# Three Strassen stages of an encoder block: products that run on in shared PSUM banks, weights two k tiles to an instruction, one weight sum by an accumulating DMA

## The chip, the core and the metric

The kernel runs on one core of a Trainium2 chip. The metric is the device time of one launch in microseconds. The engines in the text: TensorE (PE in rows; PEld is its weight load), VectorE (DVE), ScalarE (ACT), GpSimd (POOL, which here also issues some DMAs), SyncE (SP, which issues most DMAs).

## The reference

One transformer block on 512 tokens of 2048 features, in float32; the output is its final RMSNorm.

```
a = rms_norm(h);  z = a @ w_in            # 5120 columns: queries, keys, values, two gMLP halves
h = h + [diff_attention(z) | gmlp_spatial_gate(z)] @ w_out
f = rms_norm(h)
h = h + (silu(f @ ffn_w1) * (f @ ffn_w3)) @ ffn_w2      # 5632 hidden columns
h = h + (p @ pl_w_up) * sigmoid(h @ pl_w_gate)          # "gate stage" below
out = rms_norm(h, final_norm_g)
```

## The kernel before

**Split operands.** TensorE multiplies float32r. Each operand is split into a high part (ScalarE's cast, `split`, line 114) and the exact remainder (VectorE's subtraction, line 115). A product is three matmuls: high by high, low by high, high by low. The tokens' operand is stationary (128x128), the weights move past it (128x512).

**Strassen stages.** Three stages compute 2x2 blocks by Strassen-Winograd's seven products, in `winograd` (line 198): the gMLP half of w_in ("x" stage, 2 groups of 512 columns of each block), the FFN's w1 and w3 (11 groups), and the gate's matrix (`w_gate`, 2 groups). The rest (`gemm`, line 150) is plain and does not change. A group has 7 products over 8 k tiles of 128 rows, both token halves: 7 x 8 x 2 x 3 = 336 matmuls, 56 steps of 6. `steps` fixes the order: a leading product and lagging ones that use the same loaded tile, (0),(1); (2),(3,4); (5),(6). Which engine executes what in which order is this trace order, moved forward by `tc.high_priority` and held back by `following`; each engine takes its instructions strictly in order.

**What a step needs.** `prepare` (line 250) loads a 128x512 weight tile (`raw`, SP's queue), forms a weight sum where the product wants one (`sub`, line 239, VectorE), and splits into `whi`, `wlo`. It runs `ahead` steps before the product, and a tile waits until its buffer is free again. Per k tile VectorE forms four weight sums: T1 = B12 - B11, T2 = B22 - T1, T3 = B22 - B12, T4 = B21 - T2. In the x and gate stages B12 is loaded a second time for T3 (`lean`).

**What follows a product.** A product fills one PSUM bank pair `c` (128x1024). `combine` (line 350) sums them outside TensorE: two ScalarE copies, five VectorE sums with PSUM (line 346), and two sums of SBUF tiles (line 346 too, on VectorE in the x and FFN stages, on GpSimd in the gate stage, argument `urgent`). `finish` follows each block: the FFN's Silu and product, or in the gate stage (line 1004) sigmoid (L1017), times `p @ pl_w_up` (L1018), plus h (L1020), squares for the last norm (L1052), a scaling by the norm's gain of the first blocks (`scale_up`, L1069), and the final scaling and store (`final`, L1085). In the gate stage GpSimd does L1020 and L1069 and part of L1018, VectorE the rest. In the last group the last product runs one token half after the other (`late`), so that the first half can finish earlier.

**Gate stage's start.** `gate_op` builds the stationary operand of the last two pairs of k tiles from h inside the stage (L191 and L115 on VectorE, 128x256 and 128x512).

Of the kernel before, what the change touches and what calls it, by code (L numbers as in the profile page):

```python
# [19 lines left out]
P = 128  # L20
# [31 lines left out]
class Lazy:  # L52
    """The items of a list from one on, some of which are yet to come."""
# [8 lines left out]
def block_kernel(ctx: ExitStack, tc: tile.TileContext, out, xT, pT, w_in, w_vg, w_out, w13, w2,  # L62
# [16 lines left out]
    ngain = const.tile([P, KT], F32, name="ngain")  # L79
    nc.vector.tensor_scalar(out=ngain, in0=gain[:, 0], scalar1=-1.0, scalar2=None, op0=ALU.mult)  # L80
# [54 lines left out]
    def gemm(w, op, evac, pg, before=None):  # L135
        """w: DRAM [128, nk, 256]; op: nk tiles [128, 2, 512]; evac(m, psum [128, 512])."""
# [33 lines left out]
    def moving7(pool, bufs, tmp, src, scales):  # L170
        """src: [128, 2, 512], a pair of k tiles -> [128, 7, 2, 256] in the products' order."""
# [27 lines left out]
    def winograd(wps, bp, tp, pp, op, w, ahead, lean, late, done, at, extra=None):  # L199
        """w: DRAM [groups, 128, 4, 8, 512], blocks B11, B12, B21, B22; done(g, i, psum, later)  # L200
        follows the i-th product of group g; at: what else follows which step.
        op: for each pair of k tiles, (product, part, half) -> stationary [128, 128].
        lean: loads what it can again. late: the last group does the first half of the tokens first.
        extra: a plain product before it all, (operand, DRAM [n, 128, nk, 512], evac), with
        evac(n, half of the tokens, psum)."""
        ng = w.shape[0]
        steps = []
        if extra:
            eop, ew, evac = extra
            steps = [(-1, f, k) for f in range(ew.shape[0]) for k in range(ew.shape[2])]  # L210
# [15 lines left out]
        def load(src, name, bufs):  # L226
            t = (bp if name == "b12" else wps[0]).tile([P, T], F32, name=name, bufs=bufs)
# [15 lines left out]
        def halves():  # L243
            return tuple(wps[1].tile([P, T], F32R, name=n, bufs=ahead + 1) for n in ("whi", "wlo"))

        def prepare(g, i, c):
            if g < 0:
                x = load(ew[i, :, c], "raw", RAWS)
            elif i == 0:
                x = raw(g, 0, c, "raw", RAWS)  # L250
                t1 = tp.tile([P, T], F32, name="t1", bufs=KP + SKEW)
                held[c] = [t1, b12(g, c)]
            elif i in (2, 5):
                x = raw(g, 3 if i == 2 else 2, c, "raw", RAWS)
                held[c][2:] = [x]
# [928 lines left out]
```

## Time and profile before

| | us |
|---|---|
| three runs | 2266.6, 2267.86, 2268.9; median 2267.86 |
| profiled execution: span, first to last instruction | 2266.5 |
| its first stage: normalised input, queries and keys of one head | 8.7 to 87.6 |
| x stage (Strassen) | 87.6 to 244.9 |
| other columns of w_in, attention, gMLP, w_out | 244.9 to 676.1 |
| product of p, FFN's first stage (Strassen) | 676.1 to 1576.4 |
| FFN's second product | 1576.4 to 2065.9 |
| gate stage (Strassen) | 2065.9 to 2254.0 |
| last scaling and stores | 2254.0 to 2266.5 |

The profile has no time of this execution other than its span; it lies 1.4 us under the median. Stages are cut where the lines of TensorE's matmuls change. In a timeline row the bracket is the engine's idle time just ahead of it and what released it; in a wait row, A <- B says that A's engine stood until B was done.

### The profile page before, as it was taken

To read this page: it belongs to the slowest core of one execution; us is meant where nothing else is said; L and a number is where in the kernel's file an instruction comes from. 1 tells how busy PE (TensorE), PEld (TensorE's weight loads), DVE (VectorE), ACT (ScalarE), POOL (GpSimd) and SP (SyncE) were. 2 spreads that over 40 slices of the span, in tenths; PEclk is the share of its full clock that TensorE was granted. 3 is DMA by queue.
4 is the path that set the end of the run, shared out by engine and by line. 5 is a ranking of instruction groups with operands and counts; after the bars stand their busy time and mean duration, and the time that the engine had idled before them with its cause. 6 is when DMAs were issued, how large, how long until landed. Compare 5 with 4: busy or idle time off the path is not lost. (4 is left out here: it accounts for less than half of the span.)

```text
span 2266.5 us, 27314 instructions
## 1 busy us (share of the span) xinstructions
PE 2211.0 (98%) x9714; PEld 1789.6 (79%) x9714; DVE 1547.4 (68%) x2243; ACT 995.2 (44%) x1591; POOL 175.4 (8%) x166
## 2 busy tenths in 40 slices
PE   7999999999999999999999999999999999999986
PEld 5788777878887888888888888887888888887764
DVE  8688754564539888887887888788333333556888
ACT  6355333453425545545544554555222222334544
POOL 4000300001210000000000000000000000000243
PEclk9999999999999999999999999999999999999998
DMA  5455522224436443444344344433543343545554
GB/s 167 158 154 159 198 93 75 84 75 148 142 125 215 120 140 108 120 126 127 104 122 127 111 121 118 129 107 119 177 152 120 106 141 97 151 131 165 154 163 158
DMA packets 133656, 300.57 MB, mean 133 GB/s; under 512 B 14560, under 2 KB 20192, under 8 KB 133520
## 3 DMA queue, kind: packets, MB, share of 16 engines
q1 hardware_dynamic: 110384, 245.94, 36.4%
q0 software_dynamic: 8672, 30.60, 4.0%
q10 hardware_dynamic: 14464, 22.30, 2.8%
q8 instruction: 76, 1.25, 0.2%
q14 instruction: 60, 0.49, 0.1%
HBM read 265.49 MB, written 33.29 MB: 132 GB/s over the span
## 5 line engine op out<-in xcount | busy, mean ns | idle before, releaser
L314 PE MATMUL c<-whi,op 128*128 128x512 f32 x3344 | 1051.6, 396 | 4.1 <-ACT whi L114 4.1
L314 PEld LDWEIGHTS c<-whi,op 128*128 128x128 f32 x3344 | 627.4, 189 | 145.7 <-ACT whi L114 5.8
L114 ACT CAST whi<-raw 128x512 fp32r<-128x512 f32 (+1 forms) x545 | 406.1, 747 | 717.3 <-PE ps L150 437.2
L115 DVE TENSOR_TENSOR wlo<-raw,whi 128x512 fp32r<-128x512 f32 (+1 forms) x545 | 466.2, 859 | 349.7 <-ACT whi L114 343.0
L314 PE MATMUL c<-wlo,op 128*128 128x512 f32 x1680 | 663.8, 396 | 17.2 <-DVE wlo L115 17.2
L150 PE MATMUL ps<-gop,whi 128*128 128x512 f32 x1408 | 435.4, 390 | 1.0 <-DVE c L346 1.0
L314 PEld LDWEIGHTS c<-wlo,op 128*128 128x128 f32 x1680 | 316.9, 189 | 98.4 <-DVE wlo L115 26.4
L150 PE MATMUL ps<-op,whi 128*128 128x512 f32 x1088 | 346.7, 399 | 0.0
L114 ACT CAST whi<-t 128x512 fp32r<-128x512 f32 x356 | 219.5, 620 | 213.4 <-PE c L314 143.5
L150 PEld LDWEIGHTS ps<-gop,whi 128*128 128x128 f32 x1408 | 263.2, 188 | 54.8 <-ACT gop L114 1.2
L115 DVE TENSOR_TENSOR wlo<-t,whi 128x512 fp32r<-128x512 f32 x352 | 245.1, 703 | 78.5 <-ACT whi L114 76.5
L150 PE MATMUL ps<-gop,wlo 128*128 128x512 f32 x704 | 274.4, 390 | 0.8 <-DVE wlo L115 0.8
L150 PEld LDWEIGHTS ps<-op,whi 128*128 128x128 f32 x1088 | 202.5, 188 | 44.3 <-issue 2.7
L150 PE MATMUL ps<-op,wlo 128*128 128x512 f32 x544 | 214.2, 394 | 0.0
L239 DVE TENSOR_TENSOR t<-raw,t 128x512 f32<-128x512 f32 x240 | 172.8, 721 | 46.6 <-DMA raw<-w 22.4
L150 PEld LDWEIGHTS ps<-gop,wlo 128*128 128x128 f32 x704 | 132.2, 188 | 29.0 <-DVE wlo L115 1.6
L150 PEld LDWEIGHTS ps<-op,wlo 128*128 128x128 f32 x544 | 102.1, 188 | 23.4 <-issue 1.1
L346 DVE TENSOR_TENSOR c<-c,c 128x1024 f32<-128x1024 f32 x91 | 111.0, 1220 | 10.2 <-PE c L314 10.2
L114 ACT CAST whi<-b 128x512 fp32r<-128x512 f32 x120 | 74.7, 623 | 90.4 <-PE c L314 78.7
L115 DVE TENSOR_TENSOR wlo<-b,whi 128x512 fp32r<-128x512 f32 x120 | 82.8, 690 | 18.2 <-ACT whi L114 16.2
L934 POOL DMA_DIRECT2D gl<-gd x17 | 12.3, 724 | 1056.2 <-ACT whi L114 723.6
L239 DVE TENSOR_TENSOR b<-raw,b 128x512 f32<-128x512 f32 x120 | 84.4, 704 | 5.6 <-DMA b<-w_vg 3.1
(173 smaller groups left out, 1378.4 us busy)
## 6 DMA issues: line engine op xcount, KB each, us to landing
raw<-w SPq DMA_DIRECT2D x264, 256.0 KB, 2.7
raw<-w SPq DMA_DIRECT2D x64, 512.0 KB, 3.6
b<-w SPq DMA_DIRECT2D x88, 256.0 KB, 2.9
raw<-w_in SPq DMA_DIRECT2D x40, 512.0 KB, 3.6
raw<-w_out SPq DMA_DIRECT2D x32, 512.0 KB, 3.6
raw<-w_vg SPq DMA_DIRECT2D x48, 256.0 KB, 2.7
raw<-w SPq DMA_DIRECT2D x32, 384.0 KB, 3.2
raw<-w_gate SPq DMA_DIRECT2D x48, 256.0 KB, 2.8
```

What stands on the lines that cost most here:

```text
L114: recent[:] = (nc.scalar.copy(out=hi, in_=src), nc.vector.tensor_tensor(out=lo, in0=src, in1=hi.bitcast(F32), op=ALU.subtract))
L115: nc.vector.tensor_tensor(out=lo, in0=src, in1=hi.bitcast(F32), op=ALU.subtract))
L150: nc.tensor.matmul(ps[:, m], lhsT=a[:, j, ms], rhs=op[k][:, b], start=k == 0 and i == 0, stop=k == nk - 1 and i == 2)
L239: nc.vector.tensor_tensor(o, x, y, op=ALU.subtract)
L314: product[:] = [nc.tensor.matmul(acc[i][:, s], lhsT=op[c](i, x, s), rhs=y, start=c == 0 and k == 0, stop=c == KP - 1 and k == 2)]
L346: (eng or nc.vector).tensor_tensor(o, x, y, op=ALU.add)
L934: nc.gpsimd.dma_start(out=t, in_=gd[k:k + 2].rearrange("k p t -> p k t"))
```

## The change

**Order and size.** Weights come two k tiles at a time: every load, sum and split is 128x1024, and a step is 12 matmuls, 28 steps to a group. The products' order is (0,1), (2,3), (4,5), 6, the second of a pair one step behind the first; `ahead` is 2 of these steps. Buffers: three raw tiles, three pairs of halves (`nhalf`), but two pairs in the gate stage. There, the last product's halves for c of 2 and 3 lie in B12's buffers.

**Banks that run on.** With changed signs of the operands, products accumulate where another left off: 0, 2, 4, 6 in one bank pair, 1 and 3 in a second, 5 alone. So the pair of bank 0 holds in turn what c11, c12 and c21 need. ScalarE copies c11, c22, c12 after products 0, 1, 2; VectorE adds to c12, c22, c11 after 3, 4, 5; c21 is read straight from PSUM by the activation that follows.

**Weight sums.** VectorE forms three per pair. The fourth, B12 + B22, is made in B12's tile by a DMA that GpSimd issues and that adds B22 from memory to the tile (line 266 after); B12 isn't loaded twice any more.

**Gate stage.** L1018's and L1020's successors (998, 999) and `scale_up` (1045) run on VectorE, 128x1024 each; GpSimd keeps only the power of the final norm. The gains' load goes to ScalarE's queue. The buffer for GpSimd's DMA descriptors shrinks to 4096 bytes.

The core of the diff (what lies between is renaming, docstrings, buffers and signs):

```diff
         for g in range(ng):
-            for lead, lag in (((0,), (1,)), ((2,), (3, 4)), ((5,), (6,))):
-                skew = KP if late and g == ng - 1 and lead == (5,) else SKEW
-                for c in range(KP + skew):
-                    steps += [(g, i, c) for i in lead if c < KP]
-                    steps += [(g, i, c - skew) for i in lag if c >= skew]
+            for lead, lag in ((0, 1), (2, 3), (4, 5), (6, None)):
+                for c in range(kw + (lag is not None)):
+                    if c < kw:
+                        steps.append((g, lead, c))
+                    if lag is not None and c:
+                        steps.append((g, lag, c - 1))
         todo = {}
         now = 0
...
-        def halves():
-            return tuple(wps[1].tile([P, T], F32R, name=n, bufs=ahead + 1) for n in ("whi", "wlo"))
+        def halves(i=0, c=0):
+            return tuple(
+                (bp.tile([P, 2, T], F32R, name=n, tag="b12", bufs=kw) if i == 6 and late and
+                 c >= nhalf else hp.tile([P, 2, T], F32R, name=n, bufs=nhalf)) for n in ("whi", "wlo"))
...
+            if g < 0:
+                return o
+            if i == 0:
+                sub(held[c][0], held[c][1], x)
+            elif i == 2:
+                nc.gpsimd.dma_start(out=held[c][1], in_=w[g, :, 3, 2 * c:2 * c + 2],
+                                    accum_op=ALU.add)
+            elif i == 5:
                 sub(held[c][0], x, held[c][0])
-                if i == 2:
-                    if lean:
-                        held[c][1] = b12(g, c)
-                    sub(held[c][1], x, held[c][1])
-            if g >= 0 and i > 0:
...
-            multiply(0, c, hi, lo)
+                acc[i] = bank() if i in (0, 1, 5) else acc.pop(i - 2)
+
+            def multiply(s, c, whi, wlo, p):
+                for e in range(2):
+                    k = 2 * c + e
+                    for x, y in ((0, whi), (1, whi), (0, wlo)):
+                        product[:] = [nc.tensor.matmul(
+                            p, lhsT=op[k](i, x, s), rhs=y[:, e],
+                            start=k == 0 and i in (0, 1, 5) and (x, y) == (0, whi),
+                            stop=k == KP - 1 and y is wlo, skip_group_check=True)]
...
-                    done(g, i, acc[i][:, 1], later, 1)
+                kept.append((c, whi, wlo))
+                if c == kw - 1:
+                    for s in range(2):
+                        for a in kept:
+                            multiply(s, *a, acc[i][:, s])
+                        done(g, i, acc[i][:, s], later, s)
             else:
-                multiply(1, c, hi, lo)
-                if c == KP - 1:
-                    done(g, i, acc.pop(i), later)
+                for s in range(2):
+                    multiply(s, c, whi, wlo, acc[i][:, s])
+                if c == kw - 1:
+                    done(g, i, acc[i], later)
             for fn, a in at.pop(now, []) + todo.pop(now, []):
                 fn(*a)
...
         def done(g, i, acc, later, s=slice(None)):
-            if i == 0:
-                nc.scalar.copy(out=new("c11"), in_=acc)
-            elif i == 1:
-                nc.scalar.copy(out=new("c22"), in_=acc)
-            elif i == 2:
-                add(new("c21"), acc, res["c11"])
-            elif i == 3:
-                add(new("c12"), acc, res["c21"])
-                later(2, add, res["c12"], res["c12"], res["c22"], eng)
-                later(5 if g == urgent else 3, finish, g, "c12", res["c12"], later)
-            elif i == 4:
...
+            if i < 3:
+                nc.scalar.copy(out=new(("c11", "c22", "c12")[i]), in_=acc)
+            elif i < 6:
+                n = ("c12", "c22", "c11")[i - 3]
+                add(res[n], acc, res[n])
+                later(1, following if g == last else (lambda fn, *a: fn(*a)), finish, g, n, res[n],
+                      later)
+            else:
+                if s in (0, slice(None)):
+                    new("c21")
+                with tc.high_priority(10 * PRIO) if g == urgent else nullcontext():
+                    finish(g, "c21", res["c21"], later, s, acc)
 
         return done
 
...
             nc.sync.dma_start(out=h, in_=hnat[f, u])
-            parts = [(s, o[:, s], h[:, s]) for s in range(2)]
+        ends = g and n in ("c11", "c21")
+        with behind() if g and not ends else nullcontext():
+            nc.scalar.activation(t, src, AF.Sigmoid)
+        nc.vector.tensor_tensor(t, t, o, op=ALU.mult)
+        end = nc.vector.tensor_tensor(t, t, h, op=ALU.add)
+        if not ends:
+            later(2 if g else 1, both, t, u, f)
+            return
+        if n == "c11":
+            both(t, u, f)
         else:
-            parts = [(s, *ahead[u, s]) for s in (range(2) if half is None else (half,))]
...
-    def scale_up(*which):
-        for u, f in which:
-            scaled_up.add((u, f))
-            for s in range(2):
-                t = res[u, f][:, s]
-                nc.gpsimd.tensor_tensor(t, t, gains_b[f], op=ALU.mult)
...
+    def scale_up(u, f):
+        scaled_up.add((u, f))
+        t = res[u, f]
+        nc.vector.tensor_tensor(t, t, gains_b[0][:, f:f + 1].broadcast_to([P, 2, T]), op=ALU.mult)
...
-                       109: [(load_last, ((1, 1, 1),))],
-                       **{2 * i + 1: [(gate_op, (spare,))] for i in range(2)},
-                       5: [(following, (next, last))], 6: [(following, (next, last))]}):
+                      {0: [(gate_op, (spare,))] * 2,
+                       2: [(following, (next, last))], 3: [(following, (next, last))],
+                       29: [(load_gains, (0, ph, "hT", KP))],
+                       36: [(scale_up, (0, 0))], 38: [(scale_up, (0, 1))],
+                       40: [(scale_up, (1, 0))], 41: [(scale_up, (1, 1))],
+                       46: [(load_last, (0, b7, "b12", KP // 2))],
+                       51: [(load_last, (1, w7, "raw", 3))],
+                       50: [(load_gains, (2, gl, "gl", 2))]}, nhalf=2):

**VectorE inside an FFN group.** The place is where the middle products give way to product 4 (before: 2, 3 and 4 run together; after: 3 ends, 4 and 5 begin). `t1` holds T1, T2, T4 in turn, `b12` T3, `raw` a loaded block. Before:

```order
L115 TENSOR_TENSOR wlo_8007<-b12_7705,whi_8006 128x512
L115 TENSOR_TENSOR wlo_8022<-t1_7766,whi_8021 128x512
L239 TENSOR_TENSOR t1_7795<-raw_8052,t1_7795 128x512
L115 TENSOR_TENSOR wlo_8032<-raw_7966,whi_8031 128x512
L239 TENSOR_TENSOR b12_7796<-raw_8052,b12_7796 128x512
L115 TENSOR_TENSOR wlo_8042<-b12_7722,whi_8041 128x512
L115 TENSOR_TENSOR wlo_8057<-t1_7795,whi_8056 128x512
L239 TENSOR_TENSOR t1_7824<-raw_8087,t1_7824 128x512
L239 TENSOR_TENSOR b12_7825<-raw_8087,b12_7825 128x512
L115 TENSOR_TENSOR wlo_8068<-raw_7980,whi_8067 128x512
L115 TENSOR_TENSOR wlo_8078<-b12_7738,whi_8077 128x512
```

After (L236 and L345 form sums, L113 splits):

```order
L113 TENSOR_TENSOR wlo_7062<-raw_7003,whi_7061 128x1024
L113 TENSOR_TENSOR wlo_7081<-t1_6908,whi_7080 128x1024
L236 TENSOR_TENSOR t1_6796<-raw_7164,t1_6796 128x1024
L113 TENSOR_TENSOR wlo_7098<-raw_7041,whi_7097 128x1024
L113 TENSOR_TENSOR wlo_7114<-raw_7077,whi_7113 128x1024
L236 TENSOR_TENSOR t1_6818<-raw_7199,t1_6818 128x1024
L113 TENSOR_TENSOR wlo_7132<-b12_6797,whi_7131 128x1024
L236 TENSOR_TENSOR t1_6862<-raw_7235,t1_6862 128x1024
L113 TENSOR_TENSOR wlo_7148<-b12_6819,whi_7147 128x1024
L345 TENSOR_TENSOR c12_7129<-c_6886,c12_7129 128x1024
```

A weight sum of B22 with `b12` is gone from VectorE, and the sums of product 5 (L236 with `raw_7164`, `raw_7199`) stand between the splits of product 3 and of product 4.

**VectorE at the gate stage's start.** `op` is the stationary operand that `gate_op` makes, `hT` is h, `ps` TensorE's result. Before:

```order
L988 TENSOR_TENSOR hT<-ps,hT 128x512 x2
L191 TENSOR_TENSOR t_16843<-hT 128x256
L191 TENSOR_TENSOR t_16844<-hT 128x256
L191 TENSOR_TENSOR t_16843<-t_16843,hT 128x256
L115 TENSOR_TENSOR op_16849<-hT,op_16849 128x256
L191 TENSOR_TENSOR t_16844<-hT,t_16843 128x256
L239 TENSOR_TENSOR t_16870<-b_16871,raw 128x512
L115 TENSOR_TENSOR op_16849<-t_16843,op_16849 128x2x256
L115 TENSOR_TENSOR op_16849<-t_16844,op_16849 128x2x256
L115 TENSOR_TENSOR wlo<-raw,whi 128x512
L115 TENSOR_TENSOR op_16849<-hT,op_16849 128x2x256
L191 TENSOR_TENSOR t_16888<-hT 128x256
```

After:

```order
L113 TENSOR_TENSOR op_14548<-t_14542,op_14548 128x2x256
L113 TENSOR_TENSOR op_14548<-t_14543,op_14548 128x2x256
L187 TENSOR_TENSOR t_14560<-hT 128x256
L187 TENSOR_TENSOR t_14561<-hT 128x256
L187 TENSOR_TENSOR t_14560<-hT,t_14560 128x256
L113 TENSOR_TENSOR op_14566<-hT,op_14566 128x256
L187 TENSOR_TENSOR t_14561<-hT,t_14560 128x256
L113 TENSOR_TENSOR op_14566<-hT,op_14566 128x2x256
L113 TENSOR_TENSOR op_14566<-t_14560,op_14566 128x2x256
L113 TENSOR_TENSOR wlo<-t_14504,whi 128x1024
L236 TENSOR_TENSOR t_14577<-b_14578,raw 128x1024
L113 TENSOR_TENSOR wlo<-raw,whi 128x1024
```

Before, the splits of weights (`wlo`) alternate with the two operands' work; after, the first split of product 1 (`wlo<-t_14504`) comes behind all but one row of both.

**GpSimd and VectorE at the gate stage's end.** GpSimd, from the stage's start to its end, before:

```order
L346 TENSOR_TENSOR hT<-hT 128x1024 x2
L1020 TENSOR_TENSOR hT<-hT,gl 128x512 x8
L1062 DMA gb<-fgain 128x512 x2
L1069 TENSOR_TENSOR hT<-hT,gb 128x512 x8
L1062 DMA gb<-fgain 128x512 x2
L346 TENSOR_TENSOR hT<-hT 128x1024 x2
L1018 TENSOR_TENSOR hT<-hT,gl 128x512 x2
L1020 TENSOR_TENSOR hT<-hT,gl 128x512 x2
L1018 TENSOR_TENSOR hT<-hT,gl 128x512 x2
L1020 TENSOR_TENSOR hT<-hT,gl 128x512 x2
L466 TENSOR_TENSOR r<-v,mhalf 128x2
L466 TENSOR_TENSOR r<-v,mhalf 128x1 x2
```

After:

```order
L266 DMA b_15078<-w_gate 128x1024
L266 DMA b_15100<-w_gate 128x1024
L266 DMA b_15151<-w_gate 128x1024
L266 DMA b_15192<-w_gate 128x1024
L447 TENSOR_TENSOR r<-v,mhalf 128x2
L447 TENSOR_TENSOR r<-v,mhalf 128x1 x2
```

Its 28 sums and products of tiles are gone; what is new are the accumulating DMAs, four a group (the first four rows of eight are left out here). VectorE over the last product's splits, before (`lo` is `wlo` in a borrowed buffer):

```order
L115 TENSOR_TENSOR lo<-t_17562,wlo 128x512
L115 TENSOR_TENSOR lo<-t_17578,whi 128x512
L115 TENSOR_TENSOR lo<-t_17616,wlo 128x512
L346 TENSOR_TENSOR hT<-c,hT 128x1024
L115 TENSOR_TENSOR lo<-t_17656,whi 128x512
L115 TENSOR_TENSOR lo<-t_17683,wlo 128x512
L115 TENSOR_TENSOR lo<-t_17713,whi 128x512
L1018 TENSOR_TENSOR hT<-hT,last 128x512 x2
L1020 TENSOR_TENSOR hT<-hT,last 128x512 x2
L115 TENSOR_TENSOR lo<-t_17739,wlo 128x512
L1075 TENSOR_REDUCE fs<-ssq 128x2
```

After:

```order
L345 TENSOR_TENSOR hT<-c,hT 128x1024
L113 TENSOR_TENSOR wlo<-raw,whi 128x1024
L113 TENSOR_TENSOR wlo<-t_15077,whi 128x1024
L998 TENSOR_TENSOR hT<-hT,gl 128x1024
L345 TENSOR_TENSOR hT<-c,hT 128x1024
L113 TENSOR_TENSOR wlo<-t_15099,whi 128x1024
L998 TENSOR_TENSOR hT<-hT,last 128x1024
L999 TENSOR_TENSOR hT<-hT,gl 128x1024
L999 TENSOR_TENSOR hT<-hT,last 128x1024
L113 TENSOR_TENSOR wlo<-t_15191,whi 128x1024
L1051 TENSOR_REDUCE fs<-ssq 128x2
```

VectorE's rows for c11's and c22's finish (998, 999) now stand ahead of the last split, whole 128x1024 tiles each, where before only c11's, by halves, stood there.

## Rows read from the trace of the kernel before

**Rows 1.** The page, part 1: busy time and share of each engine.

```profile
PE 2211.0 (98%) x9714; PEld 1789.6 (79%) x9714; DVE 1547.4 (68%) x2243; ACT 995.2 (44%) x1591; POOL 175.4 (8%) x166
```

**Rows 2.** Stretches: length, busy us (instructions) by engine, clock, DMA share, GB/s.

```profile
700.00:1576.40 876.40, 874.52 (x3860) 710.56 (x3859) 736.36 (x1099) 451.48 (x724) 4.36 (x5) 1.00 0.41 121
...
2065.90:2130.00 64.10, 62.85 (x270) 49.42 (x269) 56.81 (x90) 33.93 (x56) 4.59 (x2) 1.00 0.52 152
2130.00:2190.00 60.00, 48.59 (x193) 36.38 (x192) 53.62 (x64) 29.48 (x58) 34.06 (x21) 0.97 0.56 179
...
2222.00:2253.60 31.60, 23.64 (x85) 15.37 (x83) 30.64 (x31) 15.66 (x32) 19.04 (x11) 0.95 0.29 93
```

**Rows 3.** Waits of TensorE in the gate stage: total, times, longest.

```profile
PE c L314 <- DVE wlo L115: 13.6, 11, 2.8
...
PE c L314 <- ACT whi L114: 4.1, 3, 2.0
...
PE c L314 <- DVE lo L115: 2.9, 4, 0.8
```

**Rows 4.** Timeline of TensorE at 2131 us: start, length, [idle before].

```profile
2133.27 0.78 PE L314 MATMUL c<-wlo,op 128*128 128x512 f32 x1 [1.85 <-DVE wlo L115]
2133.85 1.05 PE L314 MATMUL c<-whi,op 128*128 128x512 f32 x2
```

**Rows 5.** Timeline of VectorE in the gate stage, before and beside GpSimd's work.

```profile
2173.03 0.69 DVE L115 TENSOR_TENSOR wlo<-t,whi 128x512 fp32r<-128x512 f32 x1
...
2177.03 1.75 DVE L115 TENSOR_TENSOR wlo<-t,whi 128x512 fp32r<-128x512 f32 x1
```

**Rows 6.** Timeline of GpSimd in the gate stage.

```profile
2125.33 5.53 POOL L346 TENSOR_TENSOR hT<-hT 128x1024 f32<-128x1024 f32 x2 [188.91 <-ACT whi L114]
...
2171.97 14.66 POOL L1069 TENSOR_TENSOR hT<-hT,gb 128x512 f32<-128x512 f32 x8 [4.01 <-ACT whi L114]
...
2226.77 3.40 POOL L1018 TENSOR_TENSOR hT<-hT,gl 128x512 f32<-128x512 f32 x2
```

**Rows 7.** Groups by line and form, 700 to 1566 us: busy, mean ns.

```profile
L115 DVE TENSOR_TENSOR wlo<-t,whi 128x512 fp32r<-128x512 f32 x261 | 178.3, 688 | 68.9 <-ACT whi L114 67.1
...
L346 DVE TENSOR_TENSOR c<-c,c 128x1024 f32<-128x1024 f32 x75 | 91.5, 1220 | 4.6 <-PE c L314 4.5
```

**Rows 8.** Groups by line and form, 245 to 676 us.

```profile
L115 DVE TENSOR_TENSOR wlo<-raw,whi 128x1024 fp32r<-128x1024 f32 x66 | 82.1, 1244 | 102.4 <-ACT whi L114 97.9 <-PE sc L706 4.3
L114 ACT CAST whi<-raw 128x1024 fp32r<-128x1024 f32 x66 | 69.3, 1051 | 161.8 <-PE ps L150 134.7 <-issue 25.3 <-ACT lg L717 1.7
```

**Rows 9.** DMA issues: queue, count, KB each, median us to landing.

```profile
raw<-w SPq DMA_DIRECT2D x264, 256.0 KB, 2.7
raw<-w SPq DMA_DIRECT2D x64, 512.0 KB, 3.6
...
gl<-gd POOLq DMA_DIRECT2D x17, 512.0 KB, 4.4
...
z<-zqk POOLq DMA_DIRECT2D x3, 512.0 KB, 8.0
```

**Rows 10.** Timeline of TensorE where the FFN's first stage begins.

```profile
707.16 0.50 PE L314 MATMUL c<-wlo,op 128*128 128x512 f32 x1 [1.88 <-DVE wlo L115]
```

**Rows 11.** Timeline of VectorE where the gate stage begins.

```profile
2068.06 1.28 DVE L988 TENSOR_TENSOR hT<-ps,hT 128x512 f32<-128x512 f32 x2
2069.25 0.75 DVE L191 TENSOR_TENSOR t<-hT 128x256 f32<-128x256 f32 x2
...
2071.53 1.29 DVE L115 TENSOR_TENSOR op<-t,op 128x512 fp32r<-128x512 f32 x2
```

**Rows 12.** Timeline of TensorE at its end.

```profile
2253.59 0.39 PE L314 MATMUL c<-lo,op 128*128 128x512 f32 x1
```

**Rows 13.** Timeline of VectorE behind TensorE's end.

```profile
2254.53 0.68 DVE L346 TENSOR_TENSOR hT<-c,hT 128x512 f32<-128x512 f32 x1
...
2259.65 1.41 DVE L1085 SCALAR_TENSOR_TENSOR hT<-hT,r,gb 128x512 f32<-128x512 f32 x2 [0.67 <-POOL r L466]
```

More of the change, by code (lines that the diff above doesn't have):

```diff
@@ L197, in moving7_plain, with winograd @@
         return seven(o)
[L199 removed]
+    def winograd(rp, hp, bp, tp, pp, op, w, late, done, at, extra=None, nraw=3, nhalf=3):
         ng = w.shape[0]
@@ L261, in prepare @@
-            if g >= 0 and i > 0:
-                x = held[c][(0, 0, 0, 2, 1, 2, 0)[i]]
-            if late and g == ng - 1 and i == 6:
-                o = wps[1].tile([P, T], F32R, name=("whi", "wlo")[c % 2], bufs=ahead + 1), \
-                    tp.tile([P, T], F32R, name="lo", tag="t1", bufs=KP + SKEW) if c else \
-                    wps[0].tile([P, T], F32R, name="lo", tag="raw", bufs=RAWS)
-                del held[c]
-            else:
-                o = halves()
-            split(o, x)
@@ L271, in prepare @@
-            if g >= 0 and i == 0:
-                sub(t1, held[c][1], x)
+                x = raw(g, 0, c)
+                t1 = tp.tile([P, 2, T], F32, name="t1", bufs=kw)
+                held[c] = [t1, raw(g, 1, c, "b12")]
+            elif i == 2:
+                held[c].append(raw(g, 3, c))
+                add(held[c][0], held[c][2], held[c][0])
+            elif i == 5:
+                x = raw(g, 2, c)
+            if g >= 0 and i not in (0, 5):
+                x = held[c][{1: 0, 2: 0, 3: 2, 4: 1, 6: 0}[i]]
@@ L338, in rest @@
                     fn(*a)
-                if n > now + 4 and n % 2:
+                if n > now + 2:
                     yield
@@ L495, in sums @@
         def sums(c):
-            (g0, g1), n0 = (gain[:, 0, 2 * c + e:2 * c + e + 1] for e in range(2)), \
-                ngain[:, 2 * c:2 * c + 1]
+            g0, g1 = (gain[:, 0, 2 * c + e:2 * c + e + 1] for e in range(2))
             x11, x21, x12, x22 = (xs[2 * c + e][:, n:n + 256] for e in range(2) for n in (0, 256))
@@ L1002, in block_kernel, with finish @@
     ssq = const.tile([P, 4, 4], F32, name="ssq")
-    def finish(g, n, t, later, half=None):
+    def finish(g, n, t, later, half=None, acc=None):
         u, f = int(n[1]) - 1, 2 * g + int(n[2]) - 1
         res[u, f] = t
-        ends = g == 1 and n in ("c11", "c21")
-        if not ends:
+        src = t if acc is None else acc
+        if half in (0, 1):
+            t, (o, h) = t[:, half], (x[:, half] for x in ahead[u])
+        elif g and n == "c11":
+            o, h = ahead[u]
+        else:
             o, h = (gl.tile([P, 2, T], F32, name="gl", bufs=2) for _ in range(2))
@@ L1021, in finish @@
-        if ends:
-            for s, *_ in parts:
-                squares(t, u, f, s)
-            with tc.issue_after(end.ins):
-                for fn in waiting:
-                    fn()
-            waiting.clear()
-            scale = final(u, *([] if half is None else [half]))
-            if half == 0:
-                waiting.append(scale)
-            else:
-                scale()
+        ends = g and n in ("c11", "c21")
+        with behind() if g and not ends else nullcontext():
+            nc.scalar.activation(t, src, AF.Sigmoid)
@@ new lines, in finish @@
+        nc.vector.tensor_tensor(t, t, o, op=ALU.mult)
[5 more added lines that the diff above has]
+            both(t, u, f)
+        else:
+            squares(t, u, f, half)
+        with tc.issue_after(end.ins):
+            for fn in waiting:
+                fn()
+        waiting.clear()
+        scale = final(u, *([half] if half in (0, 1) else []))
+        if half == 0:
+            waiting.append(scale)
@@ L1033, in finish, with load_last @@
         else:
-            later(5 if g else 3, both, t, u, f)
+            scale()
     waiting = []
     ahead = {}
-    def load_last(*which):
-        for u, s, n in which:
-            p, tag, bufs = (b7, "b12", SKEW + 2) if u == 0 else \
-                (w7, "raw", RAWS) if s + n < 2 else (t7, "t1", KP + SKEW)
-            t = p.tile([P, T], F32, name="last", tag=tag, bufs=bufs)
-            nc.sync.dma_start(out=t, in_=(upd, hnat)[n][2, u, :, s])
-            ahead.setdefault((u, s), []).append(t)
+    def load_last(u, pool, tag, bufs):
+        ahead[u] = [pool.tile([P, 2, T], F32, name="last", tag=tag, bufs=bufs) for _ in range(2)]
+        for t, d in zip(ahead[u], (upd, hnat)):
+            nc.sync.dma_start(out=t, in_=d[2, u])
```

173 lines of the change are left out of this document (62 added, 111 removed).

## The prediction

> **What bounds the kernel now.** I read the busy table first: TensorE is busy 2211.0 of 2266.5 us [rows 1], so anything that only lightens VectorE, ScalarE or GpSimd is worth nothing where TensorE does not stand. Next the stretches of time [rows 2]: the FFN's first stage, where most of the changed work lies, has TensorE busy 874.52 of 876.40 us. Its weights could be made for nothing and at most 1.9 us would be won. The gate stage differs: 1.25 us of idle in 2065.9 to 2130, 11.41 in the next 60, and 7.96 in 2222 to 2253.6. The list of waits gives the same sum by cause: 13.6 + 4.1 + 2.9 = 20.6 us in 11 + 3 + 4 = 18 stops, 16.5 of it for VectorE's remainders [rows 3].
>
> A stop costs more than its idle time. In the first stretch 270 matmuls take 62.85 us, about 0.234 each without the stops [rows 2]. The stage has 2 x 336 = 672 matmuls, which is 157.2 us; it lasts from 2065.9 to 2254.0 [rows 12], 188.1 us, so 31 us are lost. 20.6 are the idle times. TensorE's timeline shows two matmuls in 1.05 us behind the stop at 2131 [rows 4], 0.42 apart instead of 0.234: the lower of its two clock levels, 1.2 instead of 2.4 GHz. It shows as a mean clock of 0.97 and 0.95 in the two stretches [rows 2], half a clock for some 3.4 us each, so 1.7 us lost twice. The other 7 us are 0.4 for each of 18 stops, the emptying and refilling.
>
> Why VectorE is late there: a 128x512 subtraction takes 0.69 us alone and 1.75 beside GpSimd's multiplications [rows 5], while GpSimd works on tiles at 2125, at 2172 (14.66 us without a break) and from 2221 [rows 6]. The three stretches of waiting are those.
>
> **The change part by part.** The matmuls are the same in number, form and operands' places, so TensorE's 2211 us stay. All that can move is stops, the start and the tail. SyncE issues fewer, larger loads; no wait in [rows 3] names it.
>
> *Gate stage, removed.* GpSimd's 28 operations on tiles go. Four sums (L346) are needed no more; VectorE takes over the rest, eight products and sums of 128x1024 (before in 16 halves) and four scalings. A 128x1024 operation takes 1.22 to 1.24 us [rows 7, 8]. Operations overlap by some 0.09: two L988 begin at 2068.06 and what follows at 2069.25, 0.60 each where one alone takes 0.69 [rows 11, 5]. So back to back I take 1.13. VectorE's rows of the stage are 104 such operations and about 12 us of small ones: 104 x 1.13 + 12 = 130 us against 157 of matmuls. It fits on average, so only the tight places count:
> - Start. Product 1's first remainder stands behind gate_op's two operands on VectorE. One costs five operations of 128x256 at 0.34 and three of 128x512 at 0.60 (0.75 and 1.29 for two in [rows 11], less the overlap), 3.5 us; the row order leaves 6.4 us ahead of it. The two sums with TensorE's last FFN result take 1.28 [rows 11] and end 1.5 to 3.4 us into the stage. So the remainder is there at 1.5 + 6.4 + 1.2 = 9.1 to 11.0; TensorE, with two steps of 12 x 0.234 = 2.81 and two matmuls more, needs it at 6.1. Stop: 3.0 to 4.9, taken as 3.7.
> - Product 4 in both groups. Its first remainder stands behind the sum of product 5's second tile, whose raw buffer is set free by the third tile of product 3. With two pairs of halves a split starts when the step two before it has ended; cast 1.05 [rows 8] and remainder 1.2 follow, then the load, 3.6 us (4.4 from GpSimd's queue) [rows 9], then sum and remainder. The same chain stands one tile earlier. From the end of that step: next load landed after 0.4 to 1.1, its sum 1.1 later, remainder 1.2 later, so 2.7 to 3.4; load to 6.3 or 7.8, sum and remainder to 8.6 or 10.1. TensorE needs it at 3 x 2.81 + 0.47 = 8.9. Stop: none to 1.2, with 0.4 for the stop and the gate matrix's busier DMAs (0.5 to 0.56 of their time, 0.41 in the FFN [rows 2]) 1.9; in the second group 2.7, since scale_up's operations lie just ahead.
> - End. Between the remainders of the last product's third and fourth tile stand three operations, 3 x 1.13 + 1.13 = 4.5 us; TensorE has 1.41 + 0.47 = 1.9 of work. Stop of 2.6 less what the third is early, taken as 2.0; one place earlier a sum with PSUM and a product cost 1.3.
>
> Together 3.7 + 1.9 + 2.7 + 3.3 = 11.6, and 2 for one half-clock spell and small stops: 13.6 of 31 are left, 17.4 saved. From both sides: all stops gone but the start's, 27 saved; as many as before, nothing saved.
>
> *Tail.* Before, a sum of 0.68 at 2254.53 follows the last matmul, which ends at 2254.0 [rows 12, 13]; it goes, since the sigmoid reads PSUM. With its hand-over 0.5 to 2 us are saved of 12.5; I take 1.5.
>
> *FFN stage.* VectorE's work per group falls from 736.36 / 11 = 67 us [rows 2] to about 43 x 1.13 + 3 = 52 of 79; below 100% before, it is worth none of the saving. The place before product 4 is the same as in the gate stage, with one step more, as there are three pairs of halves: the remainder is there 8.8 to 10.3 us after the step's end, TensorE needs it at 11.3. Slack 1.0 to 2.5 at a load of 3.6 to 4.4. A load that lands 1 us later makes it 2 us later, since two loads follow one another. The accumulating DMA is nowhere in this trace. Bounds: as a plain load from GpSimd's queue, 4.4, at best, and 8.0, the slowest load of that size [rows 9]; I take 4.9 for it and for the loads beside it, nearer to the first, as the stage's DMAs have half their time free. The remainder that waits for the sum is used some 8 steps (22 us) behind its issue, so its own length is hidden at both ends; what it costs is what it does to the raw loads: 2 x (4.9 - 3.6) - 2.5 = 0.1 us late, with some of the 0.4 of a stop 0.15 per group, 1.7 in all. The bounds are nothing and the first rival's price. The stage's start, a stop of 1.88 now [rows 10], stays within 0.5, and the x stage with its two groups costs 0.5.
>
> Sum: 2266.5 - 17.4 - 1.5 + 1.7 + 0.5 = 2249.8 for a profiled execution; the median of three runs lies 1.4 above it, so 2251.
>
> The page "DMA: Bandwidth & Descriptors" of the Trainium skill, section "Issuing engines are not separate DMA queues", says that DMAs begun by any engine share the same 16 DMA engines and interleave. It speaks against the change: GpSimd's queue is no road of its own. By that rule the FFN's DMA share grows and the raw loads beside the accumulating DMAs land later. The trace agrees so far as the DMAs' mean time to landing differs with the place, but no run here shows the two side by side; the rival below is priced from rows alone.
>
> **The rivals.**
> 1. *The accumulating DMAs crowd the raw loads, slower.* They are issued when B22's tiles are prepared, just when B22's last and B21's first tiles load, which is the tight chain. For it: the FFN loads 5 blocks where it loaded 4, so its DMA share goes from 0.41 [rows 2] to 0.51 or, if the read of the tile counts too, 0.6. Against: the mean share leaves room, and VectorE has 27 us of slack per group. Price: a load that lands in 5.7 to 6.1 us instead of 3.6 makes the remainder 2 x 2.1 - 2.5 = 1.7 to 2.5 us late in every group, 11 in the FFN and 2 each in the x and gate stages: 25 to 37 us in place of the 2.2 of the sum, 2274 to 2286. It decides the sign where the 17 us are eaten, at 1.3 us a group or a load of 5.5 us.
> 2. *The gate's gain is given back, no change.* VectorE now carries GpSimd's work and has two pairs of halves only; every place that is late by a step stops TensorE. For it: VectorE was busy 53.62 of 60 us there [rows 2]. Against: that was at 1.75 us an operation. Price: 25 of 31 us stay, 2266.5 - 6 - 1.5 + 2.2 + 1.4 = 2263.
> 3. *Stops nearly vanish.* If gate_op's chain starts earlier than I let it and the loads run ahead, 25 to 27 us are saved: 2266.5 - 26 - 2 + 0 + 1.4 = 2240.
> 4. *Products that run on wait for the copy of their bank.* A product that adds to a bank may not begin before ScalarE has copied what stands there (about 1.05 for 128x1024, as the cast [rows 8]). Two steps, 5.6 us, of other products lie between. If ScalarE's queue makes a copy 6 us late once a group, that is a stop of about 1 us: 15 in all, 2266. Nothing in the profile speaks for it but the 13 + 2 places.
>
> **How the numbers follow.** Forecast 0.57, rival 1 0.16 (a milder form, 1 us a group, 2262, counted with it), rival 2 0.10, rival 3 0.12, rival 4 0.05. Within 0.2% (4.5 us) is what a measurement of this kernel cannot tell from no change: 2263.3 to 2272.4. Faster: the forecast (0.56), rival 3 (0.12), half of rival 2 (0.05), a little of rival 1 (0.03): 0.76. Slower: most of rival 1 (0.11) and some of what no rival names, 0.04: 0.15. Same: the rest of the rivals, 0.09. The forecast's own range is 2244 to 2259. The range to hold 8 in 10 takes in rival 3, rivals 2 and 4 and the mild end of rival 1, and leaves out its price in full (0.1) and what lies under rival 3: 2237 to 2273.
>
> **What would show it.** In the profile after: TensorE's idle in the gate stage about 10 us, waits for `wlo` at its start, before product 4 and at its very end; no VectorE operation of 128x1024 above 1.3 us; GpSimd without work on tiles; the FFN stage within 876 to 880 us. Wrong if the FFN stage exceeds 885 us with waits behind raw loads (rival 1), if TensorE's idle in the gate stage stays near 20 us (rival 2) or falls under 5 (rival 3), or if TensorE waits for ScalarE's copies (rival 4).

## The result, and the profile after

The changed kernel takes 2280.91 us (median of four runs, 2277.84 to 2283.48) against 2267.35 before. The recorded ratio, of fast runs alone, is 1.0054, interval 1.004 to 1.0069; the quotient of these two medians is 1.0060. It is slower by some 13 us where 17 less were forecast. The profiled execution has a span of 2279.3 us, 12.8 more than that of before.

The table of busy times, the counterpart of [rows 1]:

```profile
PE 2218.6 (97%) x9714; PEld 1791.8 (79%) x9714; DVE 1346.2 (59%) x1467; ACT 931.5 (41%) x1175; POOL 168.5 (7%) x194
```

VectorE lost 201 us of work, ScalarE 64, and none of it shows in the time. The stages, cut at the first matmul of each line (and at the last of the gate stage), tell where the 12.8 us are:

| stage, us | before | after | difference |
|---|---|---|---|
| to the x stage | 87.6 | 87.5 | -0.1 |
| x stage | 157.3 | 160.5 | +3.2 |
| w_in, attention, w_out, product of p | 455.1 | 456.0 | +0.9 |
| FFN's first stage | 877.8 | 886.0 | +8.2 |
| FFN's second product | 488.2 | 489.7 | +1.5 |
| gate stage, first to last matmul | 187.7 | 189.0 | +1.3 |
| behind it | 12.9 | 10.6 | -2.3 |

These are two single executions. The x stage's code of before takes 157.3, 155.2 and 154.1 us in three traces (before, runs 4 and 7), the FFN's first stage 877.8, 879.2 and 879.4; so a difference of 2 or 3 us in one stage is not clear of noise by itself.

The gate stage was to give 17 us and gives none. The stretch of the FFN's first stage and that of the gate stage, in the columns of [rows 2], with the tail:

```profile
704.10:1590.00 885.90, 880.67 (x3861) 709.92 (x3859) 597.19 (x529) 406.57 (x435) 40.94 (x49) 1.00 0.54 146
2079.70:2269.10 189.40, 169.70 (x681) 131.13 (x679) 135.04 (x132) 88.21 (x113) 8.20 (x10) 0.94 0.56 162
2269.10:2279.30 10.20, 0.00 (x0) 0.00 (x0) 4.34 (x8) 2.65 (x5) 0.55 (x1) 0.69 0.42 155
```

GpSimd is busy 8.20 us in the gate stage, VectorE 135 of 189: both as forecast. TensorE's waits there, where [rows 3] stood:

```profile
PE c L313 <- DVE wlo L113: 14.1, 8, 6.4
...
PE c L313 <- ACT whi L112: 4.2, 1, 4.2
...
PE c L313 <- ACT hT L997: 1.3, 1, 1.3
```

There are 10 stops instead of 18, but of 19.6 us in place of 20.6, the longest of 6.4. The clock's mean of 0.94, against 0.98 over the whole stage before, says that the lower level lasts longer. What stands behind the longest stop is seen on four engines: TensorE, VectorE, and the DMA issues of GpSimd and SyncE, in the second group's first steps.

```profile
2188.35 0.79 PE L313 MATMUL c<-wlo,op 128*128 128x512 f32 x1 [6.36 <-DVE wlo L113]
```

```profile
2177.47 1.22 DVE L113 TENSOR_TENSOR wlo<-t,whi 128x1024 fp32r<-128x1024 f32 x1
2184.45 1.22 DVE L236 TENSOR_TENSOR t<-b,raw 128x1024 f32<-128x1024 f32 x1 [5.76 <-DMA raw<-w_gate]
```

```profile
2171.53 0.86 POOL L266 DMA_DIRECT2D b<-w_gate  x1 [4.82 <-ACT whi L112]
2172.67 0.87 POOL L266 DMA_DIRECT2D b<-w_gate  x1 [0.28 <-issue]
```

```profile
2173.30 2.22 SPq L228 DMA_DIRECT2D raw<-w_gate  x2
```

Two accumulating DMAs begin at 2171.53 and 2172.67, two raw loads at 2173.30 and 2175.18 (the second of that row). A raw load takes 3.6 us in [rows 9]; the first of these takes 11.1, VectorE waits for it until 2184.45, with all splits behind it, and TensorE until 2188.35. The DMA engines are full in these us (columns as in [rows 2]; a share a little above 1 is a stretch in which packets reach over its edge):

```profile
2170.00:2175.00 5.00, 5.00 (x23) 3.89 (x22) 4.34 (x4) 3.12 (x5) 1.73 (x2) 1.00 1.05 287
2175.00:2180.00 5.00, 5.00 (x23) 4.00 (x23) 3.65 (x4) 3.33 (x6) 0.00 (x0) 1.00 1.00 226
2180.00:2185.00 5.00, 1.99 (x9) 1.28 (x7) 0.55 (x1) 1.05 (x1) 0.00 (x0) 0.92 1.03 345
```

The list of DMA issues gives the medians, in the columns of [rows 9]:

```profile
raw<-w SPq DMA_DIRECT2D x196, 512.0 KB, 3.7
...
b<-w POOLq DMA_DIRECT2D x44, 512.0 KB, 5.7
...
raw<-w_vg SPq DMA_DIRECT2D x24, 512.0 KB, 4.7
...
raw<-w_gate SPq DMA_DIRECT2D x24, 512.0 KB, 4.3
...
b<-w_vg POOLq DMA_DIRECT2D x8, 512.0 KB, 9.6
...
b<-w_gate POOLq DMA_DIRECT2D x8, 512.0 KB, 6.9
```

In the FFN the raw loads land as fast as ever in the median; in the x and gate stages they are late, and there the accumulating DMAs themselves take longest. The spread of the gate's raw loads:

```profile
DMA to landing us min/median/max: 3.4/4.3/11.1
```

The start of the FFN's stage looks the same: its stop, 1.88 in [rows 10], is now 3.29. The cast that it waits for (`whi`) had stood 4.39 us for a raw tile.

```profile
719.56 0.58 PE L313 MATMUL c<-whi,op 128*128 128x512 f32 x1 [3.29 <-ACT whi L112]
```

### The profile page after: what moved, and what is told of

Same layout as the page of the kernel before. It is cut to its first block, busy times and chain, and to the rows that moved or that the text cites. A ratio compares the mean times of both kernels' runs of the same rounds, so it can differ in the third digit from the quotient of the medians.

```text
span 2279.3 us, 25011 instructions
## 1 busy us (share of the span) xinstructions
PE 2218.6 (97%) x9714; PEld 1791.8 (79%) x9714; DVE 1346.2 (59%) x1467; ACT 931.5 (41%) x1175; POOL 168.5 (7%) x194
## 4 chain that ended last, share of the span: by engine, by line
PE 85%; DMA 6%; DVE 5%; issue 2%; ACT 1%; POOL 0%; DVEq 0%; SPq 0%; POOLq 0%; ACTq 0%
PE c L313 45%; PE ps L148 36%; DVE wlo L113 2%; PE c L518 1%; DMA raw<-w_gate 1%; DMA raw<-w_vg 1%; PE pt L387 1%; DMA raw<-w 1%; PE sc L685 1%; PE pt L716 1%; DVE t L487 1%; ACT whi L112 1%; DMA gl<-gd 0%; DMA upd<-up 0%; DVE op L117 0%
## 5 line engine op out<-in xcount | busy, mean ns | idle before, releaser
L313 PE MATMUL c<-whi,op 128*128 128x512 f32 x3360 | 1063.7, 398 | 9.1 <-ACT whi L112 7.4
L313 PEld LDWEIGHTS c<-whi,op 128*128 128x128 f32 x3360 | 632.1, 189 | 156.4 <-ACT whi L112 8.9
L112 ACT CAST whi<-raw 128x1024 fp32r<-128x1024 f32 (+2 forms) x361 | 370.9, 1029 | 769.6 <-PE ps L148 439.1
L313 PE MATMUL c<-wlo,op 128*128 128x512 f32 x1680 | 665.2, 396 | 18.6 <-DVE wlo L113 18.3
L113 DVE TENSOR_TENSOR wlo<-raw,whi 128x1024 fp32r<-128x1024 f32 (+2 forms) x361 | 430.9, 1195 | 413.0 <-ACT whi L112 408.1
L313 PEld LDWEIGHTS c<-wlo,op 128*128 128x128 f32 x1680 | 317.6, 189 | 102.4 <-DVE wlo L113 29.3
L112 ACT CAST whi<-t 128x1024 fp32r<-128x1024 f32 x180 | 188.9, 1049 | 258.7 <-PE c L313 233.2
L113 DVE TENSOR_TENSOR wlo<-t,whi 128x1024 fp32r<-128x1024 f32 x180 | 218.2, 1221 | 58.6 <-ACT whi L112 57.7
L345 DVE TENSOR_TENSOR t<-raw,t 128x1024 f32<-128x1024 f32 x60 | 73.3, 1224 | 76.6 <-DMA raw<-w 54.8
L236 DVE TENSOR_TENSOR t<-raw,t 128x1024 f32<-128x1024 f32 x60 | 73.5, 1225 | 74.5 <-DMA raw<-w 55.7
L236 DVE TENSOR_TENSOR t<-b,raw 128x1024 f32<-128x1024 f32 x60 | 73.3, 1224 | 62.1 <-DMA raw<-w 37.7
L112 ACT CAST whi<-b 128x1024 fp32r<-128x1024 f32 x60 | 63.0, 1050 | 79.1 <-PE c L313 78.9
L266 POOL DMA_DIRECT2D b<-w x44 | 37.9, 861 | 739.3 <-ACT whi L112 408.6
L113 DVE TENSOR_TENSOR wlo<-b,whi 128x1024 fp32r<-128x1024 f32 x60 | 73.3, 1221 | 18.9 <-ACT whi L112 18.8
## 6 DMA issues: line engine op xcount, KB each, us to landing
raw<-w SPq DMA_DIRECT2D x196, 512.0 KB, 3.7
b<-w SPq DMA_DIRECT2D x44, 512.0 KB, 3.8
b<-w POOLq DMA_DIRECT2D x44, 512.0 KB, 5.7
raw<-w_in SPq DMA_DIRECT2D x40, 512.0 KB, 3.6
raw<-w_out SPq DMA_DIRECT2D x32, 512.0 KB, 3.7
raw<-w_vg SPq DMA_DIRECT2D x24, 512.0 KB, 4.7
raw<-w_gate SPq DMA_DIRECT2D x24, 512.0 KB, 4.3
```

What stands on the lines that cost most here:

```text
L112: recent[:] = (nc.scalar.copy(out=hi, in_=src), nc.vector.tensor_tensor(out=lo, in0=src, in1=hi.bitcast(F32), op=ALU.subtract))
L113: nc.vector.tensor_tensor(out=lo, in0=src, in1=hi.bitcast(F32), op=ALU.subtract))
L236: nc.vector.tensor_tensor(o, x, y, op=ALU.subtract)
L266: nc.gpsimd.dma_start(out=held[c][1], in_=w[g, :, 3, 2 * c:2 * c + 2], accum_op=ALU.add)
L313: product[:] = [nc.tensor.matmul(p, lhsT=op[k](i, x, s), rhs=y[:, e], start=k == 0 and i in (0, 1, 5) and (x, y) == (0, whi), stop=k == KP ...
L345: (eng or nc.vector).tensor_tensor(o, x, y, op=ALU.add)
```

## The experiments

Theory A: the accumulating DMAs take the DMA engines from the raw loads, but only in bursts, above all where a stage begins and tiles, B12 and B22 load at once. Theory B, the main rival: few buffers and VectorE's load make the stops, and the DMA is innocent. Each run stands beside runs of the kernel before on its chip (medians of 2266.4 for runs 1, 2, 4 and 7, 2268.1 for 3, 5 and 6, 2266.5 for 8); the ratios are against these. "Pitch" is the mean time from one matmul's start to the next where TensorE does not stop. A stop at a stage's start or end is counted from one matmul's start to the next, beyond the pitch, and comes out up to 0.4 us longer than the idle time in a row.

**1. The sum back on VectorE.**

```diff
-                nc.gpsimd.dma_start(out=held[c][1], in_=w[g, :, 3, 2 * c:2 * c + 2],
-                                    accum_op=ALU.add)
+                add(held[c][1], held[c][2], held[c][1])
```

> The changed kernel with the accumulating DMA taken out: B12 + B22 is summed on VectorE from the loaded tile of B22 (60 more sums of 1.13 us). Theory A, the accumulating DMAs crowd the raw loads where they come in a burst (start of the FFN's first stage, x and gate stage): raw loads of the gate matrix land in under 6 us instead of up to 11, the gate stage from first to last matmul falls from 189.0 to about 175 to 179, the FFN's start stop from 3.7 to about 2, in all 2260 to 2267. Theory B, too few buffers and VectorE's own load make the stops: the gate stage stays at 187 to 195 and the time at 2278 to 2286.

Measured: 2257.85 us, ratio 0.9962 (0.9947 to 0.9977), so 23 us less than with the DMA (22.6 by the spans), and 2 us under theory A's range. By the stages of the table: x 155.4 (5.1 less), FFN 882.2 (3.8 less), gate stage 176.2 (12.8 less), the rest within 0.7. The gate's raw loads, and TensorE's row at the place of the longest stop (2188.35 there):

```profile
raw<-w_gate SPq DMA_DIRECT2D x24, 512.0 KB, 3.7
```

```profile
2168.90 0.49 PE L312 MATMUL c<-wlo,op 128*128 128x512 f32 x1 [0.95 <-DVE wlo L113]
```

The longest of these loads takes 7.6 us, over the 6 that were expected. Theory A holds, B falls: VectorE got 60 sums more and TensorE stopped less. By groups of the gate stage, 93.2 and 96.2 us fall to 89.0 and 87.6. The stage's first two stops, idle times of 2.0 and 4.2 us, stay as they were: the DMA does not make them (run 5).

**2. The same bytes without the accumulation.** The line of run 1 is `nc.gpsimd.dma_start(out=held[c][1], in_=w[g, :, 3, 2 * c:2 * c + 2])`.

This kernel leaves B12 out of the sum, so its output is not the block's; only its time is of use.

> The changed kernel with the accumulating DMA turned into a plain load of the same 512 KB by the same queue into the same tile; it leaves out B12 in that sum. Theory A1, the price is the accumulation (3.1 us of all 16 DMA engines for 512 KB by the queue's totals, against 1.7 for a plain load): more than half of the gain of the run with the sum on VectorE, 2266 to 2273. Theory A2, the price is the fifth load itself: within 3 us of the changed kernel, 2277 to 2284. Theory B: also unchanged.

Measured: 2266.44 us (2260.67 to 2269.51), 0.9995 (0.9984 to 1.0005). Of the 23 us, 14.5 go with the accumulation and 8.6 with the fifth load. The shares differ by place: in the profiled execution the gate stage is 182.4 us, halfway between 189.0 and 176.2, the x stage 155.6, as in run 1. The longest stop is here

```profile
2178.23 0.79 PE L312 MATMUL c<-wlo,op 128*128 128x512 f32 x1 [4.26 <-DVE wlo L113]
```

so at that place most of it goes with the fifth load itself. For the accumulation's part the totals of GpSimd's queue (packets, MB, share of 16 engines over the span) give a reason; first the changed kernel, then this one, then run 1:

```profile
q0 software_dynamic: 16992, 61.01, 12.1%
```

```profile
q0 software_dynamic: 16992, 61.01, 8.6%
```

```profile
q0 software_dynamic: 8352, 29.55, 4.1%
```

60 accumulating DMAs take 8.0% of 2279.3 us, 3.0 us of all 16 engines each; as plain loads of the same bytes 4.5% of 2267.0, 1.7 us. The accumulating DMA holds the engines 1.8 times as long as the load.

**3. Accumulation in the FFN alone.** As run 1, `if ng > 2` keeps the DMA (the FFN has 11 groups, the others 2).

> The changed kernel with the accumulating DMA kept in the FFN's first stage (11 groups, 44 of its 60) and taken out of the x and gate stages, where VectorE sums. Theory A (a burst crowds the raw loads; in the FFN's steady state the loads have room): the x stage at about 155.5 and the gate stage at 176 as with the sum on VectorE everywhere, the FFN stage near the changed kernel's 886 with its start stop of 3.7, in all 2260 to 2263. Rival (every accumulating DMA costs about the same, 22.6 / 60 = 0.38 us): 44 of 60 stay, 2274.

Measured: 2264.25 us, 0.9984 (0.9975 to 0.9993). The x stage is 155.8, the gate stage 177.8, as in run 1; the FFN's is 887.5, 5.4 longer than run 1's. Its stops in the first 40 us grow from 3.2 to 6.3 us and its first group from 82.1 to 86.3; 1.2 us are left for the other ten groups. So 44 of 60 DMAs cost 6 of 23 us (5 of 22 where each time is taken against the kernel before on its chip), most of it at the stage's start. The uniform price (2274) falls; theory A holds, 1 us above its range. In the changed kernel itself the first group takes 84.1 us, 2.1 more than in run 1, and the other ten together 801.8 against 800.1, 1.7 more. How large the start's part is stays uncertain: the first group of before's code takes 80.2, 81.6 and 82.1 us in three traces.

**4. Before, with GpSimd's tile work on VectorE.** Four places of before, `nc.gpsimd` to `nc.vector`: the sums of L346, L1018, L1020, L1069.

> The kernel before with GpSimd's 28 tile operations of the gate stage put on VectorE, nothing else. Theory C, the step of the prediction: before's 31 us of stops there come of VectorE's slowing beside GpSimd (0.69 to 1.75 us), so they fall to 10 to 18 and the time to 2250 to 2258. Rival: VectorE is then late by its added work and the time stays at 2264 to 2272.

Measured: 2253.48 us, 0.9942 (0.9928 to 0.9957). The gate stage is 170.0 us, first to last matmul, 17.7 less; the tail is 4.9 longer, as VectorE comes to its last products and scalings later. VectorE's rows by form in that stage, first before, then here:

```profile
L239 DVE TENSOR_TENSOR t<-raw,t 128x512 f32<-128x512 f32 x32 | 29.6, 930 | 10.5 <-DMA raw<-w_gate 10.4
...
L346 DVE TENSOR_TENSOR hT<-c,hT 128x1024 f32<-128x1024 f32 x9 | 11.0, 1219 | 0.2 <-PE c L314 0.2
```

```profile
L239 DVE TENSOR_TENSOR t<-raw,t 128x512 f32<-128x512 f32 x32 | 22.0, 687 | 5.8 <-DMA raw<-w_gate 5.8
...
L346 DVE TENSOR_TENSOR hT<-c,hT 128x1024 f32<-128x1024 f32 x9 | 11.0, 1219 | 0.2 <-PE c L314 0.2
```

A sum of two SBUF tiles falls from a mean of 930 to 687 ns; one with PSUM stays at 1219. The prediction's reason for before's stops is shown: the stops on `wlo` come of VectorE's slowing beside GpSimd, and with GpSimd's work on VectorE itself they are fewer. VectorE's waits in that stage before name no result of GpSimd, so it is not that GpSimd's sums came late.

By the Trainium skill, "SBUF — State Buffer", section "Who interferes with whom", a VectorE instruction with two SBUF inputs contends with a GpSimd one that reads SBUF, one with a single SBUF input, outside the two-port modes, does not. The trace agrees: 930 to 687, and 1219 twice.

**5. The gate stage's start.** On run 1: gate_op at steps 1 and 2 instead of twice at 0, its temporaries in `gl`, the two calls of `following` at steps 5 and 6 instead of 2 and 3, and the stage's pools in another order:

```diff
-    w7, b7, v7, t7 = (ctx.enter_context(pool(n, bufs=1)) for n in ("w7g", "b7g", "v7g", "t7g"))
+    w7, v7, t7 = (ctx.enter_context(pool(n, bufs=1)) for n in ("w7g", "v7g", "t7g"))
+    ctx.enter_context(pool("gap", bufs=1)).tile([P, 2 * T], F32, name="gap")
+    b7 = ctx.enter_context(pool("b7g", bufs=1))
```

The reason is a row of the changed kernel that run 1 has too (2070.08 there): VectorE at the stage's first step.

```profile
2079.89 1.23 DVE L236 TENSOR_TENSOR t<-b,raw 128x1024 f32<-128x1024 f32 x1 [8.40 <-PE ps L148]
```

The first weight sum waits 8.40 us for TensorE, because its tile lies where the FFN's second product keeps its last remainder; two splits stand behind it, and then gate_op.

> The kernel with the sum on VectorE everywhere, and the gate stage's first step rearranged: gate_op one and two steps later with its temporaries in gl's buffers, and the stage's pools in another order with 4 KB left free, so that the first weight sum need not wait for memory that FFN's second product reads to its end. Theory E: the start's stops, 7.8 us instead of the prediction's 3.7, come of VectorE standing 8.4 us for that memory and of the splits behind gate_op; they fall to 1 to 4, the gate stage from 176.2 to 169 to 173, the time from 2258 to 2251 to 2255. Rival: the loads of the stage's first tiles end last anyway, and it stays at 2256 to 2260.

Measured: 2251.08 us, 0.9924 (0.9908 to 0.994). The gate stage is 169.4 us, 6.8 less than in run 1; the stops at its start fall from 7.8 to 1.3 us, and the wait of 8.40 is gone. What stays is mainly three at its end, 5 us together. Theory E holds; what the memory and what gate_op's later place give was not tried apart.

**6. TensorE's halves in turn.** On run 1, in `multiply`'s loop: `for e in range(2): for s in range(2)` instead of s outside.

> The kernel with the sum on VectorE everywhere, and in each step TensorE's 12 matmuls in the order of before (3 of one token half, 3 of the other, then the second k tile) instead of 6 and 6. Theory F: the order makes the FFN stage's mean pitch of 0.2324 us instead of before's 0.2316, and with it some 3 of the 4.4 us that the stage is longer than before's: 2254 to 2256, pitch back at 0.2316. Rival: the pitch hangs on where operands lie, and neither changes: 2257 to 2259.

Measured: 2256.3 us, 0.995 (0.9934 to 0.9966), an interval that overlaps run 1's. The FFN's stage is 879.4 instead of 882.2, its pitch 0.2320 us, between 0.2324 and before's 0.2316: 0.0004 x 3696 = 1.5 us. It shows in every group behind the first, 79.72 us instead of 79.86. The first group is 1.4 us shorter, no more than traces of the same code differ by there. Theory F is half right: the order changes the pitch, but by half of the 0.0008 that was expected, and the time lies between the two ranges.

**7. Before with aligned operands.** A tile of 32 bytes under the right side of SBUF.

> The kernel before with one 32-byte tile put under everything on the right side of SBUF, so that the stationary operands of 3270 matmuls lie at multiples of 64 bytes instead of 32 beyond one. In the trace of before matmuls whose stationary tile lies at a multiple of 64 follow each other at 0.227 us, the others at 0.234. Theory D, the address makes the pitch: 3270 x 7.5 ns = 24 us less, 2240 to 2247, and the gate stage's pitch falls to 0.227. Rival, the pitch goes with something else of these stages: 2266 to 2269.

Measured: 2266.42 us, 0.9999 (0.999 to 1.0009), the pitch in the FFN 0.2316 as before, in the gate stage 0.2334 against 0.2341, not 0.227. Theory D falls: the address modulo 64 bytes is not what makes 0.234 of 0.227. What does is open.

**8. Runs 5 and 6 together.**

> The two last edits together: the gate stage's start moved and TensorE's halves in turn, on the kernel with the sum on VectorE. If their gains are of different stages (6.8 us in the gate stage, 1.6 in the FFN), they add: 2248 to 2251, the FFN stage near 879.5 and the gate stage near 169.4. If the second was noise of the runs: 2250 to 2252, the FFN stage at 881 to 882.

Measured: 2248.11 us, 0.9922 (0.9909 to 0.9936): the FFN's stage 878.0, the gate stage 170.1. The FFN's groups behind the first take 79.72 us as in run 6, and the gate stage's start is that of run 5, so by the stages both gains are there; the ratio alone does not tell this version from run 5. It beats both kernels, by 18 us the one before.

## Why the prediction was wrong

**Removed work in the gate stage: the mechanism was right.** With GpSimd's tile work the 31 us lost to stops were to go, and 13.6 of them to come back at places of the new order: 17.4 saved. Run 4 saves 17.7 by moving that work alone. That the two numbers are so near is luck in part, since what is left in run 4 stands at places of the old order, and the changed kernel without the DMA (run 1) saves 11.5.

**The step that failed** is the accumulating DMA's price: "I take 4.9 for it and for the loads beside it, nearer to the first, as the stage's DMAs have half their time free", and with it that nearly all of its cost falls in the FFN's groups. Of the 30 us between 2251 and the measured time some 20 are this: the DMA costs 21.7 us in the three stages, and the sum had 2.2. The mean share of a stage (0.54 in the FFN after, 0.56 in the gate stage) says nothing of the 15 us or so in which the engines are full: where a stage begins and B11, B12 and B22 load at once, and in the gate's second group, where the loads for `finish` and the gains come beside (their part was not tried apart). There the gate's raw loads took up to 11 us. The bounds for the DMA itself, 4.4 to 8.0, held for the FFN (5.7) and not for the x stage (9.6); and a time to landing is the wrong measure of what it takes from others, which is engine time, 3.0 us against 1.7. The loss, by run 1: 12.8 us in the gate stage, where the sum had at most 0.4 a group for busier DMAs, 5.1 in the x stage (0.5 in the sum), 3.8 in the FFN (1.7). That the FFN's ten later groups lose 1.7 us, just what the sum had, is luck: the three stops over 0.1 us among them stand where a group begins, and none ahead of product 4.

The section that the prediction cites, "Issuing engines are not separate DMA queues" in the Trainium skill's "DMA: Bandwidth & Descriptors", said that they would interleave. The trace agrees: the gate's raw loads take 4.3 us beside the accumulating DMAs and 3.7 in run 1.

**The first rival** had the mechanism, and its range of 2274 to 2286 holds the time, but by luck: it priced 15 groups at 1.7 to 2.5 us through the chain ahead of product 4. That chain never broke: run 3's other ten groups cost 0.1 us each, and in the gate stage there is no stop ahead of product 4 in the first group and at most 0.15 us in the second, with the DMA or without (run 1), where the sum had 1.9 and 2.7. Its sign, an FFN stage over 885 us, came up with 886.0; 3.8 of that are the DMA's.

**The gate stage's other terms.** Without the DMA the stage is 176.6 us to the end of its last matmul, against the sum's 157.2 + 13.6 = 170.8. The start was mis-sized, 7.8 for 3.7: the sum let VectorE run freely up to the stage's first matmul, and it stood for memory. The two sums with TensorE's last FFN result ended 6 us into the stage where the sum had 1.5 to 3.4; in run 5 they end after 1.5. The end was 5.2 for 3.3, since TensorE also waits 1.3 us for the sigmoid that reads the bank pair's other half (`ACT hT` in the waits). Against these two, the 4.6 us ahead of product 4 did not come. The lower clock costs some 3.5 us by a mean of 0.98 over the stage (an estimate: 0.02 of 176.6), where the sum had 2 for it and small stops; what is left of the difference was not taken apart.

**FFN stage.** 8.2 us more for a forecast 1.7 + 0.5: 3.8 the DMA; 2.9 the pitch, 0.2324 for 0.2316 over 3696 matmuls, where "TensorE's 2211 us stay" was taken from number, form and operands' places; run 6 shows that half of it is the order of the token halves. The rest, 1.5 us, lies at its start and is no more than traces of the same code differ by there.

**Tail.** 1.5 less was forecast, 2.3 measured. **Banks that run on** cost no visible wait for a copy; rival 4 falls. Rival 2's sign, idle near 20 us in the gate stage, came up with 19.6, but not for its reason: in run 1 VectorE has 60 sums more and the idle is 12.6. Rival 3 falls, as the stops did not vanish.

## What to carry to other kernels

Price a DMA that replaces an engine's work by the DMA engines' time in the few us in which these are fullest, not by its landing time or by the stage's mean share. Where a stage begins, look at which tiles lie on memory that the stage before reads to its end: one sum that waits holds the whole queue behind it. An engine's 200 us of saved work are worth only what its late instructions held up.

## What the runs showed of the hardware

An accumulating DMA of 512 KB took 3.0 us of all 16 DMA engines, the plain one of the same bytes 1.7 (the changed kernel, runs 1 and 2). The pitch of a 128x512 matmul of the same types, at the full clock, was 0.227 us in the x stage and in the FFN's second product, 0.232 in the FFN's first stage and 0.233 to 0.234 in the gate stage. The order of the token halves moved it by 0.2% (0.2324 to 0.2320, run 6); 32 bytes of address did not move it in the FFN (run 7). What makes the rest is open. A VectorE sum of two SBUF tiles took 930 ns on average beside GpSimd's work on tiles and 687 without it, a sum with PSUM 1219 both times (run 4).
